# Loading and multiplying the latents' half of x ahead of the context's half in a two-layer transformer block

## The chip, the cores and the metric

The kernel runs on one core of a Trainium2 chip. The metric is the device time of one execution in microseconds (us). Engines are named as in the profile: PE is TensorE (PEld its weight loads), DVE is VectorE, ACT is ScalarE, POOL is GpSimd, SP is SyncE, which issues most loads.

## The reference, cut to what matters

Two layers run over 256 latent tokens (`x`) and 256 context tokens (`ctx`), each of width 1024. What the change touches is the head of layer 0:

```python
sh1, sc1, g1, sh2, sc2, g2 = ada_mod(c, ada_w[0], ada_b[0])          # latents
csh1, csc1, cg1, csh2, csc2, cg2 = ada_mod(c_ctx, ada_w[0], ada_b[0])  # context
h_lat = rms_norm(x, norm1_g[0]) * (1 + sc1) + sh1
h_ctx = rms_norm(ctx, norm1_g[0]) * (1 + csc1) + csh1
# na_mixer: q, k, v = split(h @ w_qkv), first for h_ctx, then for h_lat; attention; w_o
# then swiglu; then layer 1 (a gated scan) and a second swiglu, latents only at the end
```

`ada_mod` is silu(c) times a 1024 x 6144 matrix plus a bias, cut into six modulations. All is float32.

## The kernel before, in words

Activations are held turned: feature block k (128 features, k = 0 to 7) on the partitions, 512 tokens along the free axis, latents in columns 0 to 255 (`LAT`) and context in 256 to 511 (`CTX`). A float32 product is made of three matmuls of split operands (high by high, high by low, low by high), in `prod` at L410. Weights are loaded raw, and `split` makes a high part on ACT (L402) and a low part on DVE (L403).

The program is written against a framework that orders each engine's instructions when the kernel is built, by readiness in its own estimate and by place in the program, and that adds the waits. On the chip each engine takes its list in that fixed order.

`setup` does, in this order of the program: the loads of the two conditioning rows on ACT's queue (`crow`), the four 128-token tiles of `xt` on SP's queue (L93: two of `x`, two of `ctx`), some small rows of biases and gains; the sums of squares of the four tiles on ACT (L107) and one reciprocal root for all four on DVE (`rsqrt`, from L437); the 32 transposes of x on PE (L155) with copies out of PSUM (L156), and among them the eight matmuls that spread the roots over the partitions (L149, L150, copied out as `y0` at L152). Then come four quarters (`qd`). A quarter loads eight blocks of 256 KB of the modulation matrix (`ada_first`, L259) and makes shift and scale for two feature blocks (64 PE instructions at L266 in a single PSUM bank, a copy at L276, a transpose at L277, additions up to L286). It loads three blocks of 256 KB of the q, k and v weights (`w_raw`, L173), splits them, modulates two feature blocks (`modulate`: L363 on DVE, L366 on ACT, L367 on DVE, once for each half of the tokens), and multiplies (`toks`): for each of q, k and v, four token tiles of 128, six matmuls of 256 columns each, so 72 in a quarter. Results gather in six PSUM banks (`early`), two for each of q, k and v: the latents' and the context's.

SP's order is: `xt`, `ada_first` of quarter 0, `w_raw` of quarter 0, `ada_first` of quarter 1, and so on. `ada_first` has 18 buffers.

After `setup` comes `na`, with four groups of heads. Group 0 uses the `early` banks. Its norms of q and k, its table of biases `tb` (loaded by POOL's queue at L535, in pieces of 256 B) and its buffers lie in memory that `setup` held before. Meanwhile the next modulation (`ada`, tiles `ada_raw`, L298, two buffers; PE at L216) and the weights of group 1 (L395) are loaded. High and low weights of q and k have two buffers each: group 1's q weights can be split only when `setup` has done its last product with q's weights.

Of the kernel before, what the change touches and what calls it, by code (L numbers as in the profile page):

```python
# [41 lines left out]
class Block:  # L42
# [25 lines left out]
    def setup(self):  # L68
# [16 lines left out]
        with ExitStack() as ctx:  # L85
# [18 lines left out]
            ss = ip.tile([P, 4], F32, name="ss")  # L104
            junk = ip.tile([P, D], mybir.dt.bfloat16, name="junk")
            for tt in range(4):
                nc.scalar.activation(junk, xt[:, tt], AF.Square, accum_out=ss[:, tt : tt + 1])  # L107
            nc.vector.tensor_scalar(ss, ss, 1.0 / D, EPS, op0=ALU.mult, op1=ALU.add)
            y = self.rsqrt(ss)
# [6 lines left out]
            self.cols = const.tile([P, 2, P], F32, name="cols")  # L116
            cp = self.mixed()
            for j in range(2):
                nc.tensor.transpose(cp[:, j * P : (j + 1) * P], rows[:, j], self.ident)
                nc.vector.tensor_copy(self.cols[:, j], cp[:, j * P : (j + 1) * P])  # L120
# [15 lines left out]
            self.mod = [const.tile([P, 6, KT, 2], F32, name=f"mod{l}") for l in range(2)]  # L136
            self.gs = [const.tile([P, 2, KT, 2], F32, name=f"gs{l}") for l in range(2)]
            self.x = [const.tile([P, T], F32, name=f"x{k}") for k in range(KT)]
            self.hh = [const.tile([P, T], F32R, name=f"hh{k}") for k in range(KT)]
            self.hl = [const.tile([P, T], F32R, name=f"hl{k}") for k in range(KT)]  # L140

            for k in range(KT):
                if k == 4:

                    yb = self.mixed()
                    for tt in range(4):
                        t = slice(tt * P, (tt + 1) * P)
                        dg = ip.tile([P, P], F32, name="dg")
                        nc.vector.tensor_scalar_mul(dg, self.ident, y[:, tt : tt + 1])  # L149
                        nc.tensor.matmul(yb[:, t], self.ones, dg, start=True, stop=True, skip_group_check=True)  # L150
# [930 lines left out]
```

## Time and profile before

| | us |
|---|---|
| runs of the kernel | 1174.02, 1172.62 and one disturbed run of 2835.05; median 1174.02 |
| the profiled execution | 1168.13 |
| its span, first to last instruction | 1166.3 |

The profiled execution is 5.2 us shorter than the mean of the two undisturbed runs, 1173.3. PE's clock was granted in full in nearly the whole span. Times in rows are counted from the span's start.

### The profile page before, as it was taken

How to read it: one execution, taken by the hardware profiler on the slowest of the kernel's cores; microseconds unless marked ns; L12 is line 12 of the kernel's file. 1: busy time of each engine (PE TensorE's matmuls, PEld its weight loads, DVE VectorE, ACT ScalarE, POOL GpSimd, SP SyncE). 2: the span in 40 equal slices, each digit the busy share in tenths (PEclk: the TensorE clock that was granted, in tenths of full speed). 3: DMA queues.
4: the chain of work that ended last, by engine and by line, in shares of the span. 5: the costliest groups of instructions: out<-in, count | busy, mean ns of one | idle time of the engine just before them, and what ended most of it. 6: DMA issues, size and time to landing. Idle time of an engine off the chain costs nothing.

```text
span 1166.3 us, 21342 instructions
## 1 busy us (share of the span) xinstructions
PE 1138.9 (98%) x8539; PEld 987.2 (85%) x8539; DVE 778.7 (67%) x1872; ACT 501.7 (43%) x1079; POOL 74.5 (6%) x121
## 2 busy tenths in 40 slices
PE   6979989999999999999999999999999999999998
PEld 5968869887898787878887889889797988999998
DVE  4579776966697664845353778686768687556553
ACT  5356564745462232213223344434243465545442
POOL 1045331410000000000000000000000000000000
PEclk9999999999999999999999999999999999999999
DMA  9785452433337442636352651323232345564562
GB/s 330 252 211 94 118 131 73 64 130 124 107 93 229 135 170 94 230 136 216 130 194 68 199 167 46 100 74 110 73 110 74 99 175 197 182 210 158 197 217 87
DMA packets 134403, 169.23 MB, mean 145 GB/s; under 512 B 4609, under 2 KB 122273, under 8 KB 134305
## 3 DMA queue, kind: packets, MB, share of 16 engines
q1 hardware_dynamic: 132368, 164.64, 42.5%
q0 software_dynamic: 1728, 3.17, 3.2%
q8 instruction: 67, 1.10, 0.4%
q14 instruction: 32, 0.25, 0.1%
q10 hardware_dynamic: 208, 0.07, 0.0%
HBM read 166.82 MB, written 1.05 MB: 144 GB/s over the span
## 4 chain that ended last, share of the span: by engine, by line
PE 90%; DVE 4%; DMA 3%; ACT 2%; issue 1%; ACTq 0%; DVEq 0%
PE mm L410 49%; PE ax L410 28%; DMA ada_raw<-in_ada_w_dram 3%; PE ada_ps L216 2%; PE ax L651 2%; PE ax L902 1%; PE ax L613 1%; PE ax L579 1%; PE ax L637 1%; PE ax L885 1%; PE ax L580 1%; PE ada_ps L266 1%; ACT qs L569 1%; DVE w_lo L403 1%; PE ax L948 1%; PE ax L659 1%
## 5 line engine op out<-in xcount | busy, mean ns | idle before, releaser
L403 DVE TENSOR_TENSOR w_lo<-w_raw,w_hi 128x512 fp32r<-128x512 f32 (+1 forms) x448 | 272.5, 644 | 128.4 <-ACT w_hi L402 126.0
L402 ACT CAST w_hi<-w_raw 128x512 fp32r<-128x512 f32 (+1 forms) x448 | 238.0, 583 | 230.6 <-PE mm L410 100.3
L410 PE MATMUL mm<-hl,w_hi 128*128 128x256 f32 (+1 forms) x608 | 201.6, 333 | 0.0
L410 PE MATMUL mm<-hh,w_lo 128*128 128x256 f32 (+1 forms) x608 | 201.3, 332 | 0.0
L410 PE MATMUL mm<-hh,w_hi 128*128 128x256 f32 (+1 forms) x608 | 199.1, 329 | 0.0
L410 PE MATMUL ax<-hh,w_lo 128*128 128x256 f32 (+1 forms) x400 | 131.7, 330 | 0.0
L410 PE MATMUL ax<-hh,w_hi 128*128 128x256 f32 (+1 forms) x400 | 131.7, 329 | 0.0
L410 PE MATMUL ax<-hl,w_hi 128*128 128x256 f32 (+1 forms) x400 | 131.3, 328 | 0.0
L410 PE MATMUL mm<-w_hi,hh 128*128 128x256 f32 x448 | 126.3, 282 | 0.8 <-ACT hh L366 0.8
L410 PE MATMUL mm<-w_lo,hh 128*128 128x256 f32 x448 | 125.7, 280 | 0.0
L410 PE MATMUL mm<-w_hi,hl 128*128 128x256 f32 x448 | 125.5, 280 | 0.0
L410 PEld LDWEIGHTS mm<-hl,w_hi 128*128 128x128 f32 x608 | 114.1, 188 | 11.4
L410 PEld LDWEIGHTS mm<-hh,w_lo 128*128 128x128 f32 x608 | 114.0, 188 | 11.3
L410 PEld LDWEIGHTS mm<-hh,w_hi 128*128 128x128 f32 x608 | 113.8, 188 | 10.9 <-ACT hh L366 0.8
L319 DVE SCALAR_TENSOR_TENSOR ada_acc<-ada_raw,cs,ada_acc 128x1024 f32<-128x1024 f32 x63 | 79.0, 1280 | 19.4 <-DMA ada_raw<-in_ada_w_dram 19.2
L410 PEld LDWEIGHTS mm<-w_hi,hh 128*128 128x128 f32 x448 | 84.6, 189 | 5.1 <-issue 3.2
L410 PEld LDWEIGHTS mm<-w_hi,hl 128*128 128x128 f32 x448 | 84.2, 188 | 2.0 <-issue 1.6
L410 PEld LDWEIGHTS mm<-w_lo,hh 128*128 128x128 f32 x448 | 84.2, 188 | 1.8 <-issue 1.4
L410 PEld LDWEIGHTS ax<-hh,w_hi 128*128 128x128 f32 x400 | 75.2, 188 | 7.6 <-ACT w_hi L402 0.8
L410 PEld LDWEIGHTS ax<-hl,w_hi 128*128 128x128 f32 x400 | 75.1, 188 | 7.4
L410 PEld LDWEIGHTS ax<-hh,w_lo 128*128 128x128 f32 x400 | 74.9, 187 | 7.4 <-DVE w_lo L403 0.2
L696 ACT CAST mid_h<-sa 128x512 fp32r<-128x512 f32 (+1 forms) x44 | 22.5, 512 | 92.8 <-DVE sa L693 92.8
(278 smaller groups left out, 2133.3 us busy)
## 6 DMA issues: line engine op xcount, KB each, us to landing
w_raw<-in_ffn_w_in_dram SPq DMA_DIRECT2D x44, 1024.0 KB, 5.1
ada_raw<-in_ada_w_dram SPq DMA_DIRECT2D x80, 512.0 KB, 4.6
w_raw<-in_hg_w_in_dram SPq DMA_DIRECT2D x20, 1024.0 KB, 4.8
w_raw<-in_na_w_qkv_dram SPq DMA_DIRECT2D x9, 1024.0 KB, 5.0
ada_first<-in_ada_w_dram SPq DMA_DIRECT2D x32, 256.0 KB, 5.9
w_raw<-in_ffn_w_out_dram SPq DMA_DIRECT2D x8, 896.0 KB, 4.5
w_raw<-in_ffn_w_out_dram SPq DMA_DIRECT2D x8, 768.0 KB, 4.3
w_raw<-in_ffn_w_out_dram SPq DMA_DIRECT2D x8, 640.0 KB, 4.3
```

Of the source, the lines that this page charges most:

```text
L216: nc.tensor.matmul(ps[32 * j : 32 * j + 32, 0:256], cs[:, k, :], w[:, j * 256 : (j + 1) * 256], start=(k == 0), stop=(k == last), tile_pos ...
L266: nc.tensor.matmul(ps[32 * j : 32 * j + 32, 0:P], self.cs[:, k, :], w[:, j // 2, (j % 2) * P : (j % 2 + 1) * P], start=(k == 0), stop=(k = ...
L319: eng.scalar_tensor_tensor(acc[s], w, c, acc[s], op0=ALU.mult, op1=ALU.add)
L402: self.nc.scalar.copy(wh[:, ks], raw[:, ks])
L403: self.nc.vector.tensor_tensor(wl[:, ks], raw[:, ks], wh.bitcast(F32)[:, ks], op=ALU.subtract)
L410: self.nc.tensor.matmul(out, a, b, start=(start and i == 0 and j == 0), stop=(stop and i == n - 1 and j == 2), skip_group_check=True,)
L569: nc.scalar.activation(cap(qa[half], P - 1, back), src, AF.Copy, scale=self.q_gain[own])
L579: nc.tensor.matmul(ps, qs[a][:, t], ks[a][:, kr], start=True, stop=False, skip_group_check=True)
L580: nc.tensor.matmul(ps, self.ql[a][:, t], ks[a][:, kr], start=False, stop=True, skip_group_check=True)
L613: nc.tensor.transpose(tp[:, kt * P : (kt + 1) * P], sb[:, kt * P : (kt + 1) * P], self.ident)
L651: nc.tensor.matmul(o[64 * a : 64 * a + 64, 0:256], v[:, kt, j * P + 64 * a : j * P + 64 * a + 64], pts[a][0][:, kt], start=(kt == 0), stop ...
L696: nc.scalar.copy(mh, sa)
```

## The change

The two tiles of `ctx` are loaded after the first quarter's modulation blocks and weights, not ahead of them. Squares, root, transposes and spreading are done half by half in a new function `x_turned`: the latents' ahead of the small rows' transposes, the context's inside the first quarter, through PSUM banks that will later hold the context's products. Each quarter's products go first over the latents for q, k and v, then over the context. In quarters 1 to 3 the modulation's matmuls run over the eight blocks from the last to the first. Buffers, weights and arithmetic stay.

```diff
-            for tt in range(4):
-                src = self.in_x if tt < 2 else self.in_ctx
-                nc.sync.dma_start(xt[:, tt], src[0, (tt % 2) * P : (tt % 2 + 1) * P, :])
+            def x_in(half):
+                src = self.in_ctx if half else self.in_x
+                for i in range(2):
+                    nc.sync.dma_start(xt[:, 2 * half + i], src[0, i * P : (i + 1) * P, :])
+
+            x_in(0)
...
+            def x_turned(half, bank):
+                r = HALVES[half][1]
+                ss = ip.tile([P, 2], F32, name="ss", tag=f"ss{half}")
+                junk = ip.tile([P, D], mybir.dt.bfloat16, name="junk", tag="junk")
+                for i in range(2):
+                    nc.scalar.activation(junk, xt[:, 2 * half + i], AF.Square, accum_out=ss[:, i : i + 1])
+                nc.vector.tensor_scalar(ss, ss, 1.0 / D, EPS, op0=ALU.mult, op1=ALU.add)
+                y = self.rsqrt(ss)
+                for k in range(0, KT, 2):
+                    tp = bank()
+                    for b in range(4):
+                        last = nc.tensor.transpose(
+                            tp[:, b * P : (b + 1) * P],
+                            xt[:, 2 * half + b % 2, (k + b // 2) * P : (k + b // 2 + 1) * P],
+                            self.ident,
+                        )
+                    for e in range(2):
+                        nc.any.tensor_copy(self.x[k + e][:, r], tp[:, e * 256 : (e + 1) * 256])
+                yb = bank()
+                for i in range(2):
+                    dg = ip.tile([P, P], F32, name="dg", tag="dg", bufs=2)
+                    nc.vector.tensor_scalar_mul(dg, self.ident, y[:, i : i + 1])
+                    nc.tensor.matmul(
+                        yb[:, i * P : (i + 1) * P], self.ones, dg, start=True, stop=True, skip_group_check=True
+                    )
+                nc.scalar.copy(y0[:, r], yb[:, 0:256])
+                return last
+
+            with self.tc.issue_after(x_turned(0, self.mixed).ins):
...
             self.early = [[self.bank(t) for _ in range(2)] for t in ("mm", "ax0", "ax1")]
+            spare = [banks[1] for banks in self.early] + [self.mm()]
+            turn = iter(spare + spare[:1])
             self.ada_first(ip, 0)
             for qd in range(4):
...
                     self.split(wh, wl, raw, ks)
+                if qd == 0:
+                    x_in(1)
+                    x_turned(1, lambda: next(turn))
                 for k in (2 * qd, 2 * qd + 1):
                     for s, r in HALVES:
                         self.modulate(0, 0, k, s, r, y0[:, r])
                 if qd < 3:
                     self.ada_first(ip, qd + 1)
-                for (raw, wh, wl), banks in zip(ws, self.early):
-                    for tt in range(4):
-                        i = tt % 2
-                        self.toks(
-                            banks[tt // 2][:, i * 256 : (i + 1) * 256], (wh, wl), tt, (2 * qd, 2 * qd + 1),
-                            qd == 0 and i == 0, qd == 3 and i == 1,
-                        )
+                for half in range(2):
+                    for (raw, wh, wl), banks in zip(ws, self.early):
+                        for i in range(2):
+                            self.toks(
+                                banks[half][:, i * 256 : (i + 1) * 256], (wh, wl), 2 * half + i,
+                                (2 * qd, 2 * qd + 1), qd == 0 and i == 0, qd == 3 and i == 1,
+                            )
...
     def ada_first(self, ip, qd):
...
+            tiles.append((k, w))
+
+        for n, (k, w) in enumerate(tiles if qd == 0 else tiles[::-1]):
             for j in range(4):
                 nc.tensor.matmul(
...
-                    start=(k == 0),
-                    stop=(k == KT - 1),
+                    start=(n == 0),
+                    stop=(n == KT - 1),
```

## Rows read from the trace of the kernel before

**Rows 1.** The page, its first part: busy us (share) xinstructions by engine.

```profile
PE 1138.9 (98%) x8539; PEld 987.2 (85%) x8539; DVE 778.7 (67%) x1872; ACT 501.7 (43%) x1079; POOL 74.5 (6%) x121
```

**Rows 2.** Windows view: stretch, busy us (xcount) by engine, clock, DMA share, GB/s.

```profile
21.38:33.00 11.62, 11.62 (x116) 9.81 (x116) 7.97 (x21) 5.05 (x10) 0.00 (x0) 1.00 1.09 359
54.50:62.75 8.25, 8.25 (x73) 8.12 (x72) 4.18 (x7) 4.37 (x8) 0.00 (x0) 1.00 0.11 28
62.75:75.00 12.25, 9.23 (x90) 7.42 (x90) 9.77 (x50) 3.86 (x7) 4.92 (x9) 1.00 1.04 273
75.00:88.00 13.00, 9.96 (x76) 6.26 (x76) 9.63 (x30) 8.43 (x15) 7.53 (x8) 1.00 0.82 207
```

**Rows 3.** Chain of waits in time order, 43 to 87 us: start, us, what.

```profile
43.90 1.88 PE ada_ps L266 x64
...
57.29 5.53 PE ax L410 x48
63.45 4.90 DMA ada_raw<-in_ada_w_dram
...
69.09 9.64 DMA ada_raw<-in_ada_w_dram
```

**Rows 4.** Timeline, SP alone: start, us, what issued xcount.

```profile
4.20 5.81 SPq L259 DMA_DIRECT2D ada_first<-in_ada_w_dram  x8
10.62 1.78 SPq L173 DMA_DIRECT2D w_raw<-in_na_w_qkv_dram  x3
12.79 5.39 SPq L259 DMA_DIRECT2D ada_first<-in_ada_w_dram  x8
...
42.93 17.99 SPq L395 DMA_DIRECT2D w_raw<-in_na_w_qkv_dram  x3
```

**Rows 5.** DMA issues from 4.1, 12.7, 60, 69 and 72 us: KB, us to landing.

```profile
ada_first<-in_ada_w_dram SPq DMA_DIRECT2D x1, 256.0 KB, 6.4
...
ada_first<-in_ada_w_dram SPq DMA_DIRECT2D x1, 256.0 KB, 5.8
...
w_raw<-in_na_w_qkv_dram SPq DMA_DIRECT2D x1, 1024.0 KB, 6.6
...
ada_raw<-in_ada_w_dram SPq DMA_DIRECT2D x1, 512.0 KB, 9.6
...
ada_raw<-in_ada_w_dram SPq DMA_DIRECT2D x1, 512.0 KB, 7.5
```

**Rows 6.** Timeline, 8 to 22 us: start, us, what xcount, [idle before, releaser].

```profile
8.54 1.06 ACT L107 ACTIVATE junk<-xt 128x1024 bf16<-128x1024 f32 x1 [1.84 <-DMA xt<-in_ctx_dram]
...
11.11 0.17 DVE L437 TENSOR_SCALAR rq_y<-ss 128x4 int32<-128x4 int32 x1
...
13.37 0.15 DVE L441 SCALAR_TENSOR_TENSOR rq_y<-rq_b,rq_y 128x4 f32<-128x4 f32 x1
...
14.22 0.71 PE L155 MATMUL mm<-ident,xt 128*128 128x128 f32 x5
...
15.86 0.49 PE L150 MATMUL mm<-dg,ones 128*128 128x128 f32 x2
...
18.62 0.29 DVE L276 COPY ada_row<-ada_ps 128x128 f32<-128x128 f32 x1 [0.89 <-PE ada_ps L266]
...
19.70 0.69 DVE L403 TENSOR_TENSOR w_lo<-w_raw,w_hi 128x512 fp32r<-128x512 f32 x1
...
20.82 0.91 ACT L366 ACTIVATE hh<-ht,mod 128x256 fp32r<-128x256 f32 x2 [1.82 <-DVE ht L363]
...
21.38 0.38 PE L410 MATMUL mm<-w_hi,hh 128*128 128x256 f32 x1 [0.77 <-ACT hh L366]
```

**Rows 7.** Waits of SP's queue, 56 to 90 us: total, times, longest us.

```profile
SPq L395 <- DVE w_lo L403: 12.5, 1, 12.5
```

**Rows 8.** DMA queues, 63 to 88 us: packets, MB, share of 16 engines.

```profile
q1 hardware_dynamic: 2680, 5.11, 60.4%
q0 software_dynamic: 384, 0.79, 30.8%
```

More of the change, by code (lines that the diff above doesn't have):

```diff
@@ L114, in setup @@
             nc.vector.tensor_tensor(self.cs[:, :, 0:2], self.cs[:, :, 0:2], cv, op=ALU.mult)
[L116 to L120, printed above, removed]
+            self.mod = [const.tile([P, 6, KT, 2], F32, name=f"mod{l}") for l in range(2)]
+            self.gs = [const.tile([P, 2, KT, 2], F32, name=f"gs{l}") for l in range(2)]
@@ new lines, in setup @@
+            self.x = [const.tile([P, T], F32, name=f"x{k}") for k in range(KT)]
+            self.hh = [const.tile([P, T], F32R, name=f"hh{k}") for k in range(KT)]
+            self.hl = [const.tile([P, T], F32R, name=f"hl{k}") for k in range(KT)]
+            y0 = ip.tile([P, T], F32, name="y0")
+            def x_turned(half, bank):
[25 more added lines that the diff above has]
+                return last
@@ L121, in setup @@
+            with self.tc.issue_after(x_turned(0, self.mixed).ins):
+                self.cols = const.tile([P, 2, P], F32, name="cols")
+                cp = self.mixed()
+                for j in range(2):
+                    nc.tensor.transpose(cp[:, j * P : (j + 1) * P], rows[:, j], self.ident)
+                    nc.vector.tensor_copy(self.cols[:, j], cp[:, j * P : (j + 1) * P])
             c0, c1 = self.cols[:, 0], self.cols[:, 1]
@@ L134, in setup @@
             nc.vector.tensor_scalar_mul(self.nomlb, self.omlb, -1.0)
[L136 to L150, printed above, removed]
-                    y0 = ip.tile([P, T], F32, name="y0")
-                    nc.scalar.copy(y0, yb)
-                tp = self.mixed()
-                for tt in range(4):
-                    nc.tensor.transpose(tp[:, tt * P : (tt + 1) * P], xt[:, tt, k * P : (k + 1) * P], self.ident)
-                nc.any.tensor_copy(self.x[k], tp)
             wq = self.in_na_w_qkv[0]
@@ L182, in setup @@
                     self.ada_first(ip, qd + 1)
-                for (raw, wh, wl), banks in zip(ws, self.early):
-                    for tt in range(4):
-                        i = tt % 2
-                        self.toks(
-                            banks[tt // 2][:, i * 256 : (i + 1) * 256], (wh, wl), tt, (2 * qd, 2 * qd + 1),
-                            qd == 0 and i == 0, qd == 3 and i == 1,
-                        )
+                for half in range(2):
[5 more added lines that the diff above has]
+                            )
     def masks(self):
@@ L256, in ada_first @@
         ps = self.psum.tile([P, T], F32, tag="ada", name="ada_ps", bufs=1)
+        tiles = []
         for k in range(KT):
```

5 lines of the change are left out of this document (removed).

## The prediction

> **What bounds the kernel now.** I read the page's first part, then the windows by stage, then the chain of waits over the first 90 us, then SP's queue. PE is busy for 1138.9 of 1166.3 us [rows 1], so a change at the head can give back only what PE loses there; whatever is gained must still be there when the long, PE-filled part begins, at about 88 us. The reader is to see three stretches in [rows 2, 3]. Up to 21.38 us PE waits for data: the first product starts then [rows 6]. From 21.38 to 62.75 us PE is never idle (11.62 busy of 11.62, 8.25 of 8.25) [rows 2]. From 62.75 to 88 us it idles again, 3.0 us in the first 12.25 and 3.0 in the next 13 [rows 2], and the chain there is made of `ada_raw` loads: 4.90 us, then 9.64 [rows 3]. In the last stretch of `setup` the DMA engines stand nearly still, 0.11 busy; behind it they are full, 1.04 [rows 2].
>
> **Loads at the head.** Block 1 of quarter 0 lands at 4.20 + 6.4 = 10.6 us, block 1 of quarter 1 at 12.79 + 5.8 = 18.6 [rows 4, 5]. Between them lie 11 loads of 256 KB in 8.0 us: 0.73 us each, 2.9 us for a megabyte. So quarter 0's last block lands at 10.6 + 7 x 0.73 = 15.7, its third weight block at 17.9, quarter 1's last block at 23.7, quarter 2's at 31.7. Taking a megabyte of `ctx` from ahead of quarter 0 moves its last block to 12.8 and its weights to 15.0. The `ctx` tiles then land at 16.4 and 17.9; everything behind lands as before.
>
> **The first product.** Before, PE's modulation is done near 18.6, where the copy starts, 2.9 us after the last block has landed: it stands in PE's list among x's transposes and the spreading of the roots. From the copy to the first product are 21.38 - 18.62 = 2.8 us, of which one DVE split of 0.69 lies in the way [rows 6]. After, PE has only half of x's turning to do and is done with it while blocks land. Eight instructions of the last block are 1.88 / 8 = 0.24 us [rows 3], so the copy starts at 13.1 and the first product comes at 15.2 to 15.9. The third weight block wants 15.0 plus a rounding and a split, about 1.3, so I take **16.0**, 5.4 us sooner.
>
> **What now lies behind it.** A quarter is 72 products at 5.53 / 48 = 0.115 us [rows 3]: 8.3 us, of which the latents' 36 are 4.15. The context's 16 transposes, at (0.71 - 0.27) / 4 = 0.11 with 0.27 for one alone, are 1.8 us, and two spreadings of 0.49 each 1.0 [rows 6]. Those 2.8 us were hidden by the waiting for blocks; now they stand behind the first product. Quarter 1's modulation is 1.9 [rows 3]. The context's chain: second tile landed 17.9; its square 1.06 and the reading of the sum, 19.2; root 13.52 - 11.11 = 2.4 plus one step, 21.8; two spreadings one after the other 1.0; a copy, a DVE and an ACT step of about 0.45 each: **24.2**. The latents' products end at 20.1, the transposes at 21.9, the spreadings near 22.8, so PE waits about 1 us for quarter 1's last block (23.7) and the context. Then 1.9 and 4.15: quarter 0 is done at **29.8**, with both orders of the last two. ACT and DVE have quarter 0's splits and both modulations in the same stretch, so 1 us of queueing may come on top.
>
> **The reversed order.** Before, quarter 1's blocks are multiplied as they land, between products: 21.38 to 33.0 is 11.6 us for 8.3 of products and 1.2 of modulation (40 of 64 instructions), so the changing to and fro costs about 2.1. One run of 64 saves most of that, and it is in the 29.8. Where it costs: the whole run now waits for the block that lands last. For quarter 2 that is 31.7, while PE arrives at 30 to 31; I take 1 us. With it quarter 1 starts about 31 + 1, against 33.0 + 1.9 less what was already done. The gain G that reaches the end of `setup` is then **2.0 us** (29.8 against 33.0 is 3.2, less 1.2 of queueing and waiting). Bounds: at best the first product comes at 15.2 and PE never waits, 15.2 + 4.15 + 2.8 + 1.9 + 4.15 = 28.2, G = 4.8; at worst, see the second rival, G = -1.5. `setup` ends at 62.8 - 2.0 = 60.8.
>
> **Where it goes next.** Two things were waiting for `setup`. POOL's table loads and the next `ada_raw` tiles wait for its end: they come 2.0 sooner. But the third `w_raw` of group 1 waits for DVE, 12.5 us [rows 7]: its raw buffer is free when q's weights of group 1 are split, and those can be split when the last product with group 0's q weights is done. Before, q's 24 products of the last quarter came first and ended at 57.29, 5.53 us ahead of the end; that load was issued at 42.93 + 17.99 - 0.38 = 60.54 [rows 3, 4], 3.25 later. After, q's context products come after all the latents', and only k's and v's context products follow: 24 x 0.115 = 2.8 us ahead of the end. The load goes out at 60.8 - 2.8 + 3.25 = **61.25**, 0.7 us *later* than before, although `setup` ends sooner. From there to the landing of the sixth `ada_raw` tile (issued at about 72.45, 7.5 to land [rows 5]: 80.0) the DMA engines are full [rows 2]. They have the same work to do: SP's queue holds 60.4% and POOL's 30.8% of them [rows 8]. Work that starts all at once at 61.25 to 61.6 and takes as long as before ends 0.7 us later, and PE, which has the modulation of these tiles in its list ahead of group 1's products, waits for them. In numbers the shift at 80 us is 2.8 - G - 0.1, about **+0.7 us**: a gain at the head of less than 2.7 is given back here. G = 4.8 makes it -2.1, G = -1.5 makes it +4.2.
>
> **A rule against the trace.** The 9.6 us of the fifth `ada_raw` tile against 4.9 of the third [rows 3, 5] show that loads of SP and of POOL hold each other up. The Trainium skill says, in "DMA: Bandwidth & Descriptors", section "Queues, rings and completion order", that each DMA engine takes turns between the queues that have work, a packet from each; by that rule table loads that start 2 us sooner delay the megabyte that now starts beside them, which puts the shift on the same side as the sum above, and the rows here agree.
>
> **Rest.** All that follows is PE's list with the same products, so the shift of 0.7 stays: 1168.13 + 0.7 = 1168.8 for the profiled execution. The two undisturbed runs lie at 1173.3 in the mean, 5.2 above it; on their scale that is **1174.0 us**. Buffers, instruction counts and arithmetic outside `setup` are the same; what differs there is only how the scheduler interleaves, worth the few tenths by which single waits in [rows 6] move, and more in 62 to 88 us, where PE's 6 us of idle time bound it: I allow 2 us either way.
>
> **Rivals.**
> *The gain is kept* (0.25). If the stage behind `setup` is not full but a chain of single loads, each issued when PE frees a buffer, all of it moves with the end of `setup`: G of 2 to 4 is kept, 1169 to 1171.5. For it: the chain of waits shows loads following PE there. Against it: DMA 1.04 and the load of 9.64 where a free one takes 4.9 [rows 2, 3].
> *The latents queue behind the context, slower* (0.13). The text of the program has `x_turned(1)` ahead of the first `modulate`, and ACT and DVE take their lists in order. If the context's squares stand ahead of the latents' `hh` on ACT, the latents wait for `ctx`: first product 19.2 + 1 = 20, G near 0, and 1176. If all of the context's turning stands ahead, the first product comes at 24.2 and 8.3 + 1.9 follow, 34.4, G = -1.5: 1177.5. The point that decides: whether the last of the context's squares starts ahead of the first `hh`. Against it: before, the list had each ready piece first (splits between the modulation's copy and `ht`) [rows 6].
> *The clock falls in the new gap* (0.07). From 13.1 to 16 PE has little to do but one transpose. If the granted clock were to fall to its lower level (1.2 GHz of 2.4), products would take 0.23: the latents' 4.15 become 8.3, of which 1 to 2 hide in the wait for the context; G about 0, 1176. Against it: the clock stays at 1.00 through 62.75 to 75 with a quarter of it idle [rows 2]. The Trainium skill's page "TensorE: Matmul & The Clock Gate", Part 1, has the rule that an idle PE is put back to half clock and must earn the full one again; no row here shows it fall.
> *The head does not move* (0.05): the load that was taken away is made up by the wait of new loads for the rows' small ones, G = 0.5, then 1175.5.
>
> **How the numbers follow.** Forecast 0.5, 1172 to 1176 by its own bounds; rivals as above. The range has the kept gain's slower three quarters on one side and the slower rivals up to 1177.5 on the other, with the 0.7 us by which the two undisturbed runs differ from their mean: 1167 to 1178.5, leaving out 2 in 10. Over 2%, about what a measurement of this kernel can tell from no change, would be 23.5 us. No case comes near: 0.02 on each side for a re-ordering of later stages, which all depend on how the scheduler lists them, and 0.96 within.
>
> **What would show it.** In the changed kernel's profile: `ctx` issued behind the first `w_raw`; the first product at 15.5 to 17; the end of `setup` at 59 to 62; the third `w_raw` of group 1 issued within 1 us of 60.5; the first `ada_raw` chain up to 88 us ending within 1.5 us of before. Wrong if the sixth tile's landing moves with `setup`'s end, if the first product comes after 19, if the windows show a clock under 1.00 in 13 to 25 us, or if later stages take another number of us for the same products.

## The result, and the profile of the changed kernel

The changed kernel takes 1181.66 us in the median (1179.35 to 1182.71, five runs) beside 1172.62 us for the kernel before on the same occasion: a ratio of 1.0083, with an interval of 1.0055 to 1.0112. It is slower by 9 to 10 us (6 to 13 by the interval). The forecast was 1174.0 with a range to 1178.5, so the time lies outside it, though within the 2% that held 0.96 of the chance. Two things went worse than the forecast said: the head of the kernel lost time, and the same products took longer in most stages. One went better, in the stage behind `setup`. The slower products have nothing to do with the order of the work.

The page's first part answers to [rows 1]:

```profile
PE 1155.0 (98%) x8539; PEld 1003.1 (85%) x8539; DVE 777.8 (66%) x1886; ACT 501.1 (42%) x1085; POOL 74.4 (6%) x121
```

PE has the same 8539 instructions and is busy for 16.1 us longer than in [rows 1], more than the 14.6 us by which the profiled span grew (1166.3 to 1180.9). So the loss isn't waiting alone: the same instructions take longer. A part of that is the clock, as the windows by stage show (columns as in [rows 2]):

```profile
13.30:18.00 4.70, 1.33 (x5) 0.88 (x5) 3.27 (x13) 3.77 (x8) 0.00 (x0) 0.72 1.03 384
18.00:26.30 8.30, 5.31 (x25) 4.94 (x25) 5.01 (x20) 3.29 (x9) 0.00 (x0) 0.71 1.10 361
26.30:32.50 6.20, 6.17 (x74) 5.33 (x75) 3.92 (x8) 2.42 (x5) 0.00 (x0) 0.50 1.10 357
54.50:68.95 14.45, 14.45 (x124) 14.32 (x124) 3.63 (x8) 3.32 (x7) 0.00 (x0) 1.00 0.01 2
...
76.50:84.70 8.20, 3.25 (x22) 2.34 (x22) 7.26 (x40) 0.60 (x1) 1.68 (x1) 0.73 1.05 270
84.70:90.50 5.80, 5.80 (x30) 4.99 (x31) 0.00 (x0) 0.00 (x0) 4.72 (x7) 0.50 0.93 223
```

The seventh column of numbers is the granted clock. In the kernel before it was 1.00 in all of these stretches. Here it is 0.72, 0.71 and 0.50 from 13.3 to 32.5 us, and 0.73 and 0.50 again from 76.5 to 90.5. Each fall comes in a stretch in which PE stood still for long: it was busy for 1.33 us of 4.70, 5.31 of 8.30, 3.25 of 8.20; the stretch behind it is then paid at half speed. The fourth row is the last stretch of `setup`: PE is full, the DMA engines stand still (0.01).

The last of these falls can't be laid to the change. Of the twenty kernels profiled for this document, the kernel before is the only one without a fall between 70 and 91 us; e17 below, with the same lists of instructions, has one, and so has e1, with nearly the same. The kernel before from 62 to 100 us:

```profile
62.00:100.00 38.00, 31.81 (x261) 23.63 (x259) 31.55 (x115) 19.71 (x41) 19.72 (x26) 1.00 0.82 197
```

And e1_rev_only:

```profile
62.00:100.00 38.00, 32.41 (x249) 24.99 (x247) 30.33 (x108) 18.64 (x39) 19.72 (x26) 0.91 0.83 194
```

Of 91 later runs of the kernel before, only 11 have a mean clock of 1.000. So its profile is of a better execution than most, and the 14.6 us between the profiled spans overstate the loss of 9 to 10 us between the medians.

What PE waited for from 12 to 100 us (us in total, times, longest):

```profile
PE ada_ps L236 <- DMA ada_raw<-in_ada_w_dram: 4.9, 2, 2.9
PE ada_ps L301 <- DVE ada_row L300: 2.7, 1, 2.7
PE mm L434 <- ACT hh L390: 2.2, 2, 1.5
PE mm L145 <- DVE dg L144: 1.5, 1, 1.5
```

DVE's own list says why. This is its timeline (start, us, what, [idle before]); the answers in [rows 6] are the copy of `ada_row` and the split next to it:

```profile
14.12 0.69 DVE L427 TENSOR_TENSOR w_lo<-w_raw,w_hi 128x512 fp32r<-128x512 f32 x1 [3.69 <-ACT w_hi L426]
14.73 0.28 DVE L156 COPY cols<-mm 128x128 f32<-128x128 f32 x1
14.93 0.68 DVE L427 TENSOR_TENSOR w_lo<-w_raw,w_hi 128x512 fp32r<-128x512 f32 x1
...
15.67 0.28 DVE L300 COPY ada_row<-ada_ps 128x128 f32<-128x128 f32 x1
...
16.93 0.48 DVE L387 SCALAR_TENSOR_TENSOR ht<-x,gs,y 128x256 f32<-128x256 f32 x1
...
20.71 0.16 DVE L461 TENSOR_SCALAR rq_y<-ss 128x2 int32<-128x2 int32 x1
...
23.70 0.48 DVE L144 TENSOR_SCALAR dg<-ident,rq_y 128x128 f32<-128x128 f32 x2
25.25 0.88 DVE L387 SCALAR_TENSOR_TENSOR ht<-x,gs,y 128x256 f32<-128x256 f32 x2 [1.07 <-ACT y L148]
```

PE has multiplied the last block at 13.27, so the copy of `ada_row` could start then. In DVE's fixed list two splits, a copy of `cols` and two small operations stand ahead. DVE stands idle for 3.69 us until the first split has its weights, and the copy starts at 15.67. Only feature block 0 of the latents is modulated at once (`ht` at 16.93, first product at 18.01). Block 1 of the latents, which needs nothing of the context, stands behind the context's copies, its root and its spreading, at 25.25. Nine products came in between, and then PE stood still twice for 1.5 us.

The chain of waits from 40 to 95 us, which answers to [rows 3] (start, us, what):

```profile
56.05 10.49 issue
66.54 0.63 ACT w_hi L426
...
69.72 0.37 SPq L419
70.18 0.53 SPq L322
70.83 13.80 DMA ada_raw<-in_ada_w_dram
```

SP's wait from 12 to 100 us, which answers to [rows 7] (total, times, longest):

```profile
SPq L419 <- DVE w_lo L427: 23.5, 2, 17.8
```

`setup` ends at 69.0 instead of 62.8, and the third `w_raw` of group 1 goes out at 69.72 instead of 60.55. It waited 17.8 us for DVE's splits, which waited for q's last products. All loads of the next stage start there, and PE waits for `ada_raw`.

Everything up to here is at the head and right behind it. That it is not all is seen in the middle of layer 0's swiglu, where nothing was edited. The chain of waits there is PE alone; before, 24 products of 512 columns:

```profile
426.11 5.49 PE mm L410 x24
```

and after, 48 of them:

```profile
425.00 11.24 PE ax L434 x48
```

5.49 / 24 is 229 ns for one product, 11.24 / 48 is 234, with the clock at 1.00 in both.

### The profile page after: what moved, and what is told of

Same layout as the page of the kernel before. It is cut to its first block, busy times and chain, and to the rows that moved or that the text cites. A ratio compares the mean times of both kernels' runs of the same rounds, so it can differ in the third digit from the quotient of the medians.

```text
span 1180.9 us, 21372 instructions
## 1 busy us (share of the span) xinstructions
PE 1155.0 (98%) x8539; PEld 1003.1 (85%) x8539; DVE 777.8 (66%) x1886; ACT 501.1 (42%) x1085; POOL 74.4 (6%) x121
## 2 busy tenths in 40 slices
DMA packets 134403, 169.24 MB, mean 143 GB/s; under 512 B 4608, under 2 KB 122272, under 8 KB 134304
## 3 DMA queue, kind: packets, MB, share of 16 engines
q0 software_dynamic: 1728, 3.17, 3.1%
## 4 chain that ended last, share of the span: by engine, by line
PE 89%; DVE 4%; DMA 3%; ACT 2%; issue 1%; SPq 0%; ACTq 0%
PE mm L434 48%; PE ax L434 29%; PE ax L675 2%; DMA ada_raw<-in_ada_w_dram 2%; PE ada_ps L236 1%; PE ax L637 1%; PE ax L603 1%; DVE w_lo L427 1%; PE ax L926 1%; PE ax L604 1%; PE ax L661 1%; PE ax L909 1%; PE ada_ps L290 1%; PE ax L972 1%; PE ax L683 1%
## 5 line engine op out<-in xcount | busy, mean ns | idle before, releaser
L434 PE MATMUL mm<-hl,w_hi 128*128 128x256 f32 (+1 forms) x584 | 196.8, 337 | 0.0
L434 PE MATMUL mm<-hh,w_lo 128*128 128x256 f32 (+1 forms) x584 | 195.9, 336 | 0.1
L434 PE MATMUL mm<-hh,w_hi 128*128 128x256 f32 (+1 forms) x584 | 194.3, 333 | 0.0
L434 PE MATMUL ax<-hl,w_hi 128*128 128x256 f32 (+1 forms) x424 | 139.2, 329 | 0.0
L434 PE MATMUL ax<-hh,w_lo 128*128 128x256 f32 (+1 forms) x424 | 139.1, 329 | 0.0
L434 PE MATMUL ax<-hh,w_hi 128*128 128x256 f32 (+1 forms) x424 | 138.9, 329 | 0.0
L434 PEld LDWEIGHTS ax<-hh,w_hi 128*128 128x128 f32 x424 | 79.6, 188 | 8.5 <-ACT hh L390 0.4
L434 PEld LDWEIGHTS ax<-hl,w_hi 128*128 128x128 f32 x424 | 79.7, 188 | 8.2
L434 PEld LDWEIGHTS ax<-hh,w_lo 128*128 128x128 f32 x424 | 79.7, 188 | 8.2
L434 PE MATMUL ax<-mid_h,w_hi 128*128 128x256 f32 (+1 forms) x222 | 72.8, 328 | 0.0
```

Of the source, the lines that this page charges most:

```text
L434: self.nc.tensor.matmul(out, a, b, start=(start and i == 0 and j == 0), stop=(stop and i == n - 1 and j == 2), skip_group_check=True,)
```

## The experiments

All ratios are to the kernel before on the same occasion, with a 95% interval. The table counts along PE's list of 4608 products with `hh` or `hl`: the end of number 287 is the end of `setup`, number 1152 is the first of layer 0's swiglu. The columns "288 to 1152" (the stage `na`) and "1152 to last" run from start to start, in us. "512" is the mean spacing of products 1632 to 1728 (512 columns, first swiglu), "256" that of 216 to 287 (last quarter of `setup`).

| kernel | ratio | `setup` ends | 288 to 1152 | 1152 to last | 512, ns | 256, ns |
|---|---|---|---|---|---|---|
| before | 1 | 62.8 | 259.7 | 775.1 | 228.9 | 114.7 |
| changed | 1.0083 | 69.0 | 261.8 | 780.4 | 234.2 | 119.3 |
| e1_rev_only | 1.0000 | 62.4 | 263.8 | 774.9 | 228.9 | 114.7 |
| e2_half_only | 0.9975 | 63.4 | 258.2 | 775.0 | 228.9 | 116.5 |
| e3_after_wm | 1.0143 | 67.2 | 264.3 | 780.9 | 234.2 | 117.9 |
| e4_after_lat | 1.0059 | 64.9 | 260.6 | 782.7 | 234.2 | 118.0 |
| e9_after_addr | 0.9990 | 67.7 | 259.6 | 773.2 | 228.9 | 115.0 |
| e10_before_addr | 1.0101 | 63.5 | 265.8 | 782.1 | 234.2 | 119.3 |
| e16_lat_addr | 0.9963 | 62.3 | 260.2 | 772.5 | 228.9 | 114.9 |
| e11_lat_addr_warm | 0.9928 | 60.6 | 259.8 | 773.0 | 228.9 | 115.0 |

The 259.7 us of the kernel before in `na` are those of its better execution, without a fall of the clock in the stage. At its pace e1 has 263.8 and e17 (below, with the same lists) 264.4, so the stage behind `setup` is best held against e1.

### One part of the change alone

The first theory, A in the expectations, had three parts: lists at the head, the clock, and q's weights held by the new product order. **e1_rev_only** is the kernel before with the reversed runs of `ada_first` alone.

```diff
-            for j in range(4):
...
+            tiles.append((k, w))
+
+        for n, (k, w) in enumerate(tiles if qd == 0 else tiles[::-1]):
```

> The kernel before with one part of the change alone: ada_first's matmuls of quarters 1 to 3 are written in the reverse order of their loads, everything else as before. Theory A (the loss comes from the engines' lists at the head, from the clock that falls in the gaps they leave, and from q's weights being held) has nothing here: 1173 us within 2, `setup` ends at 62 to 63.5 us, the granted clock is full from 12.3 us on. Rival B (the reversed run waits for its last block while the products stand behind it in TensorE's list, and that is the loss): `setup` ends at 65 or later, the clock at half in 20 to 33 us, and the median is 1178 to 1182.

1169.91 us, ratio 1.0000 [0.9981, 1.0018]: the reversal neither costs nor gives anything that lasts. Its first product comes at 21.8 and `setup` ends at 62.4; rival B falls.

**e2_half_only** has the new product order alone, and **e12_half_again** repeats it on another occasion.

```diff
-                for (raw, wh, wl), banks in zip(ws, self.early):
-                    for tt in range(4):
+                for half in range(2):
+                    for (raw, wh, wl), banks in zip(ws, self.early):
+                        for i in range(2):
```

> The kernel before with one other part alone: the products of each quarter half by half (q, k, v for the latents, then q, k, v for the context), loads, turn and ada_first as before. Theory A: the head is as before (first product about 21.4 us, clock full from 12.3), `setup` ends within 1 us of 62.75, but q's second half of weights comes free about 5 us later than before (near 60 us), so the third w_raw is issued at 60.5 to 63 and the time is 1173 to 1177. Rival C (the held weights are the whole loss): the third w_raw later than 65 us, PE idle by 3 us or more in 76 to 85 us, and 1179 to 1182.

> The kernel before with the half-by-half product order alone, a second time, on the chip of these runs, so that it can be held against the run above: 1166 to 1169 us, with product 1200 to the last in 768 us. If its earlier 0.9975 was chance, 1170 to 1172.

1167.26 us, 0.9975 [0.9955, 0.9995], and 1167.82 us, 0.9963 [0.9941, 0.9986]. Both theories had this order as a cost; it is a gain of 3 to 4 us. The hold itself is as predicted: the third `w_raw` goes out at 63.91, where the prediction's own rule (end of `setup`, 63.4, less 2.8, plus 3.25) gives 63.9. But it isn't paid for. The stage behind is shorter than in e1, 258.2 against 263.8. Product 576 still starts 0.3 us later than in e1 (135.5 against 135.2), product 672 starts 5.4 us sooner (167.0 against 172.4). PE's waits from 140 to 170 us show one place. The kernel before:

```profile
PE ada_ps L216 <- DMA ada_raw<-in_ada_w_dram: 3.2, 2, 2.6
```

And e2:

```profile
PE ax L637 <- DVE sbc L586: 0.3, 1, 0.3
```

A wait of 3 us near 154 us is gone. The other kernels of the old product order that were profiled have that wait (e1, e6, e10, e13, e15, e17: 1.2 to 3.7 us from 155 to 158 on), and in four of them (e1, e6, e10, e17) the clock is granted at half for some us from 157 to 161 on. So the place of the gain is shown. That the order of the lists in `na` brings the loads forward is only argued; which instruction does it was not followed further.

**e3_after_wm** puts the old product order back into the changed kernel.

```diff
-                for half in range(2):
-                    for (raw, wh, wl), banks in zip(ws, self.early):
+                for (raw, wh, wl), banks in zip(ws, self.early):
+                    for tt in range(4):
```

> The changed kernel with the old product order (q for all four row blocks, then k, then v), everything else as changed. Theory A: the head stays as in the changed kernel or is worse, since q's context products now stand ahead of k's latent products: the gaps and the half clock stay (clock at 1.2 GHz somewhere in 15 to 33 us), `setup` ends at 67 to 70 us, but q's weights come free some 5 us ahead of the end, so the wait at 76.5 to 84.7 us shrinks to under 1.5 us and the clock doesn't fall there: 1176 to 1179. Rival C: the head doesn't matter and the time is back at 1172 to 1174.

1185.92 us, 1.0143 [1.0108, 1.0177]: 4 us worse than the changed kernel by the medians and 7 by the ratios, where theory A had it 3 to 5 better. `setup` does end 1.8 us sooner, but the stage behind takes 264.3 instead of 261.8 and has its wait near 161 us. So the held weights are not the loss.

### The order at the head

**e4_after_lat** traces the latents' two `modulate` calls of quarter 0 first and puts the context's turn behind them.

```diff
-                    x_turned(1, lambda: next(turn))
-                for k in (2 * qd, 2 * qd + 1):
-                    for s, r in HALVES:
-                        self.modulate(0, 0, k, s, r, y0[:, r])
+                    for k in (0, 1):
+                        hh, hl = self.modulate(0, 0, k, 0, LAT, y0[:, LAT])
+                    with self.tc.issue_after(hh), self.tc.issue_after(hl):
+                        x_turned(1, lambda: next(turn))
+                    for k in (0, 1):
+                        self.modulate(0, 0, k, 1, CTX, y0[:, CTX])
```

> The changed kernel with one order changed: the latents' modulation of blocks 0 and 1 is traced ahead of the context's squares, root and turn, and these are put behind it on VectorE and ScalarE. Theory A: all 18 latent products of quarter 0 (times 2 blocks: 36) run in a row from about 17.5 to 22.5 us, the gap before 25 us shrinks from 3 us to under 1.5, the second fall of the clock (25.65 to 32.48 in the changed kernel) is gone or shorter, `setup` ends at 64 to 67 us and the time is 1175 to 1179. Rival D (the clock falls whatever the order, because the engine stood still before 16 us): the clock is at half in two stretches as in the changed kernel, `setup` ends at 68 or later, 1180 to 1183.

1177.14 us, 1.0059 [1.0036, 1.0082]. `setup` ends at 64.9, 4.1 us sooner, the waits of 1.5 us are gone, and one of the two falls of the clock with them (half from 18.1 to 24.9 only). The order is a cause, worth 4 us at the head; e5 and e7 below, timed on one occasion, confirm it in the whole time. The wait for `ada_row` stays (3.0 us), and no run moved that copy ahead of the splits: what it costs is read from the trace alone. But the swiglu stages still take 782.7 us for the same products, against 775.1 before, and no theory so far had that.

### Where the operands lie

The change needs `x`, `hh` and `hl` sooner and so allocates them ahead of `cols`, `q_gain`, `omlb` and `nomlb`. That moves them by 1184 bytes in every partition: `hh0` from byte 37440 to 36256, while `w_hi` stays at 86784 and 94976. 36256 is no multiple of 64, so the first guess was alignment. **e5_after_pad** and **e6_before_unal** put 32 bytes ahead of `x` and 32 behind `hl`, in the changed kernel and in the one before; **e7_after_lat_pad** adds e4's order.

```diff
+            const.tile([P, 8], F32, name="pad0")
             self.x = [const.tile([P, T], F32, name=f"x{k}") for k in range(KT)]
             self.hh = [const.tile([P, T], F32R, name=f"hh{k}") for k in range(KT)]
             self.hl = [const.tile([P, T], F32R, name=f"hl{k}") for k in range(KT)]
+            const.tile([P, 8], F32, name="pad1")
```

> The changed kernel with 32 bytes a partition put ahead of the tiles x, hh and hl and 32 behind them, and nothing else. In the kernel before hh0 lies at byte 37440 of a partition, a multiple of 64; the change makes these tiles ahead of cols, so hh0 lies at 36256, 32 off a multiple of 64. Theory E (address): products are paced 231 ns at 512 columns and 114 at 256 columns before, 234 and 119 after, because of that offset; with the padding the pace of before returns, the stretch from product 1200 to the last product falls from 773.5 us to 768, and the median from 1181.7 to 1175 to 1176.5. Rival F (the pace comes from the order in which PSUM banks are taken, which is shifted too, or from the chip): the pace stays at 234 and the time at 1180 to 1183.

> The kernel before with the same 32 bytes ahead of x, hh and hl and 32 behind: order, loads and banks as before, hh0 now at 37472, 32 off a multiple of 64. Theory E: 512-column products at 234 ns, product 1200 to the last in 773 to 774 us, `setup` ends 0.5 to 1.5 us later, and the median is 1175.5 to 1178. Rival F: nothing moves, 1169 to 1172.

> The changed kernel with the latents' modulation ahead of the context's turn, and with the padding. Theories A and E together: the gain of the order (4.5 us) and that of the address (5.5 to 6.5) add: 1170 to 1172.5, still with one fall of the clock near 18 to 25 us, `setup` ends at 63.5 to 65. Rival G (the gains don't add, the weights of group 1 end last whatever the head does): 1174 to 1177.

e5: 1180.53 us, 1.0089 [1.0067, 1.0111], products at 233.3 ns: not mended. e6: 1179.04 us, 1.0080 [1.0060, 1.0099], 233.3 ns: the kernel before, with no instruction in another place, is slower by 0.8% through 64 bytes of padding. So addresses matter, and a multiple of 64 is not the rule. e7: 1176.39 us, 1.0053 [1.0033, 1.0073]; the order's gain is there (every run of e7, 1174.0 to 1176.8, is faster than every run of e5, 1179.3 to 1180.7), the address's isn't.

The clean pair swaps the addresses alone: **e9_after_addr** is the changed kernel with the small tiles allocated ahead again, **e10_before_addr** the kernel before with `mod`, `gs`, `x`, `hh` and `hl` ahead of `cols`. Every engine's list is that of its parent.

```diff
+            self.cols = const.tile([P, 2, P], F32, name="cols")
+            self.q_gain = const.tile([P, 1], F32, name="q_gain")
+            self.omlb = const.tile([P, 16], F32, name="omlb")
+            self.nomlb = const.tile([P, 16], F32, name="nomlb")
             self.mod = [const.tile([P, 6, KT, 2], F32, name=f"mod{l}") for l in range(2)]
```

> The changed kernel with cols, q_gain, omlb and nomlb allocated ahead of mod, as they were before: every engine's list is that of the changed kernel, and x, hh, hl and the rings of weights lie at the addresses of the kernel before (hh0 at 37440, w_hi at 86784 and 94976). Theory E2 (the pace hangs on where the operands lie, though not on a multiple of 64 alone): 512-column products at 229 ns again, product 1200 to the last in 768 us, and 1174 to 1177 us, 5 to 6 under the changed kernel. Rival F (the order of the banks, or the order of work): 233 to 234 ns, 773 us, 1180 to 1183 us.

> The kernel before with mod, gs, x, hh and hl allocated ahead of cols, so that they lie where the change puts them (hh0 at 36256); every engine's list is that of the kernel before. Theory E2: 512-column products at 234 ns, product 1200 to the last in 773 to 774 us, 1175 to 1180 us. Rival F: 229 ns, 768 us, 1169 to 1172 us.

e9: 1170.48 us, **0.9990** [0.9971, 1.0009]. e10: 1183.67 us, **1.0101** [1.0074, 1.0128]. The chain of waits in the first swiglu, e9:

```profile
419.99 10.99 PE ax L434 x48
```

The same of e10:

```profile
423.37 11.24 PE ax L410 x48
```

229 and 234 ns have changed places, and both times lie outside theory E2's ranges, e9 under its 1174 us and e10 over its 1180. The whole 9 to 10 us by which the changed kernel is slower go away with the old addresses, and the new addresses alone put them on the kernel before. With the old addresses the change is neither faster nor slower. Of the 10.7 us between the spans of the changed kernel and e9, 7.2 lie in the swiglu and scan stages, 2.2 in `na` and 1.3 in `setup`.

Three more runs moved one operand each. **e13_before_w64**: 64 bytes behind `hl`, so the weights lie later. **e14_after_q32**: the changed kernel with `q_gain` alone ahead of `mod`, so `hh` lies 32 bytes later. **e15_before_m64**: `nomlb` behind `hl`, so `hh` lies 64 bytes earlier. **e17_before_all64** then moved `hh` and the weights by 64 together.

```diff
             self.hl = [const.tile([P, T], F32R, name=f"hl{k}") for k in range(KT)]
+            const.tile([P, 16], F32, name="pad")
```

This is e13; e17 has the same line ahead of `self.mod`. In e14 and e15 one line changes its place:

```diff
+            self.q_gain = const.tile([P, 1], F32, name="q_gain")
             self.mod = [const.tile([P, 6, KT, 2], F32, name=f"mod{l}") for l in range(2)]
...
-            self.q_gain = const.tile([P, 1], F32, name="q_gain")
```

```diff
-            self.nomlb = const.tile([P, 16], F32, name="nomlb")
...
             self.hl = [const.tile([P, T], F32R, name=f"hl{k}") for k in range(KT)]
+            self.nomlb = const.tile([P, 16], F32, name="nomlb")
```

> The kernel before with 64 bytes put behind hl: x, hh and hl stay (hh0 at 37440), the rings of weights and all that follows lie 64 bytes later (w_hi at 86848 and 95040, no longer multiples of 128). Theory J (the weights' address matters too, so the padding of the earlier runs spoiled one operand while it mended the other): 512-column products at 232 to 234 ns and 1175 to 1180 us. Rival K (only hh's and hl's address matters): 229 ns and 1169 to 1172 us.

> The changed kernel with q_gain alone allocated ahead of mod: x, hh and hl lie 32 bytes later (hh0 at 36288, a multiple of 64 and not of 128, as 37440 is), the weights and all else where the change has them. Theory J (multiples of 64 for hh and hl and multiples of 128 for the weights are enough): 229 ns, product 1200 to the last in 765 to 768 us, 1168 to 1172 us. Rival L (it is the distance between the operands or a larger block of addresses that counts): 232 to 234 ns and 1178 to 1182 us.

> The kernel before with nomlb allocated behind hl: x, hh and hl lie 64 bytes earlier (hh0 at 37376, a multiple of 128), weights as before. If a multiple of 64 is enough for hh, 229 ns and 1169 to 1172 us. If a multiple of 128 is better still, under 228 ns and 1160 to 1168. If the distance to the weights counts, 232 to 234 ns and 1175 to 1182.

> The kernel before with 64 bytes ahead of mod: x, hh, hl, the weights and all that follows lie 64 bytes later, so the distance from hh0 (37504) to w_hi (95040) is 57536 bytes as in the kernel before. The last two address runs, one with the weights 64 later and one with hh and hl 64 earlier, have the same distance of 57600 and the same pace (226.7, 120.0 and 119.2 ns). Theory M (the distance between the two operands of a product sets the pace): 228.9 ns at 512 columns, 117.8 in the last stage, 114.7 in the last quarter of `setup`, as before, and 1168 to 1172 us. Rival N (the place of either operand counts by itself): another pace, 1174 us or more.

The chain of e13 in the first swiglu:

```profile
419.48 10.88 PE ax L411 x48
```

Of e15:

```profile
419.81 10.88 PE ax L410 x48
```

Of e14:

```profile
421.89 11.20 PE ax L434 x48
```

And of e17:

```profile
419.17 10.99 PE ax L411 x48
```

| kernel | `hh0`, `w_hi` | distance | 512, ns | 256 in the last stage, ns | 256 in `setup`, ns | ratio |
|---|---|---|---|---|---|---|
| before | 37440, 94976 | 57536 | 228.9 | 117.8 | 114.7 | 1 |
| e17_before_all64 | 37504, 95040 | 57536 | 228.9 | 117.8 | 115.1 | 1.0025 [1.0008, 1.0043] |
| e13_before_w64 | 37440, 95040 | 57600 | 226.7 | 120.0 | 119.2 | 1.0075 [1.0050, 1.0100] |
| e15_before_m64 | 37376, 94976 | 57600 | 226.7 | 120.0 | 119.2 | 1.0057 [1.0038, 1.0075] |
| e14_after_q32 | 36288, 94976 | 58688 | 233.3 | 113.3 | 117.6 | 1.0038 [1.0022, 1.0055] |
| changed | 36256, 94976 | 58720 | 234.2 | 117.3 | 119.3 | 1.0083 |

None of the first three came out in full as a theory had it: e13 and e15 have a faster pace at 512 columns and lose time all the same, and e14 has the slow pace of rival L and loses only 0.4%. Its 32 bytes take back about half of the change's loss. Moving the weights 64 bytes up and moving `hh` 64 bytes down give the same pace, to a tenth of a nanosecond in three places; moving both together gives the pace of the kernel before, to 0.4 ns in the third. So, in the kernel before, the pace of a run of products went with the distance between its two operands and not with the place of either. The distance 57600 is better than that of before where `hh` streams with 512 columns and worse with 256 columns, and it loses on the whole. What is left open is the rule that turns a distance into a pace, and what in the chip does it. e17's 1.0025 is small but not quite nothing. The distance isn't all, either. e4 has the addresses of the changed kernel and from product 1152 on the same list of PE, yet it has 120.0 ns in the last stage for 117.3, and 782.7 us from there to the last for 780.4. In the same way e5 (233.3 ns at 512 columns) and e7 (232.4) share 58752. And each kernel has one profile, so whether its pace changes from one execution to the next is not shown.

### The clock

**e8_lat_pad_warm** is e7 with TensorE kept busy where it stood: 12 products behind quarter 0's `ada_first` and 4 behind its transposition. **e11_lat_addr_warm** has the same with the old addresses, **e18_lat_addr_warm_again** repeats it, and **e16_lat_addr** is e11 without the added products.

```diff
+        if qd == 0:
+            for _ in range(12):
+                nc.tensor.matmul(self.warm[:, 0:P], self.ones, tiles[-1][1][:, 0, 0:P],
+                                 start=True, stop=True, skip_group_check=True)
         row = self.spool.tile([P, 256], F32, name="ada_row", tag="ada_row", bufs=1)[:, 0:P]
```

> The same with TensorE kept busy where it stood: 12 products of ones with the last ada_first block behind the ada_first matmuls, and 4 of ones with ada_row behind the transposition, all into a bank that is written over later; they add work and nothing to the result. Theory H (the clock falls because TensorE stood still near 14 to 17 us): the granted clock stays full through 12 to 33 us and the products of quarter 0 run at 0.12 us; `setup` ends 1.5 to 3.5 us earlier than without, at 61 to 63 us, and the median is 1167 to 1170. Rival I (the clock falls for another reason, such as the small share of the array that ada_first's 32-row matmuls use): the clock falls as before and the time is that of the run without, or up to 1 us above it.

> The changed kernel with the latents' modulation ahead of the context's turn and the addresses of the kernel before, without the added products that kept TensorE busy. If the fall of the clock near 17 to 25 us costs what the pair at the other addresses showed (2.6 us), it is 1166.5 to 1169 us, with one stretch at half clock before 33 us and `setup` ending 1 to 3 us later than with the added products (60.3 for product 287). If the clock costs nothing that lasts, 1163.5 to 1165.5.

> The changed kernel with all three repairs: the latents' modulation ahead of the context's turn, TensorE kept busy from 13 to 17 us by 16 added products, and the addresses of the kernel before. If the three causes are the whole loss, `setup` ends at 60.5 to 62 us (1 to 2 ahead of before), the pace is 229 ns and the median is 1165 to 1169. If something of the change still costs (q's weights held, so that group 1 comes late), it is 1170 to 1172.5 with a wait for ada_raw of over 4 us in 70 to 90 us.

> The fastest version so far (the latents' modulation ahead of the context's turn, TensorE kept busy, the addresses of the kernel before) a second time beside the kernel before on another occasion: 1162 to 1167 us and a ratio of 0.990 to 0.996. If the first result was a lucky chip, 0.997 or above.

The windows of e7 (columns as in [rows 2]):

```profile
12.50:17.70 5.20, 1.69 (x13) 0.87 (x13) 3.67 (x13) 2.56 (x6) 0.00 (x0) 0.86 1.05 384
17.70:23.50 5.80, 5.74 (x28) 5.74 (x29) 4.55 (x19) 3.62 (x9) 0.00 (x0) 0.54 1.10 348
```

And of e8:

```profile
12.50:19.50 7.00, 6.57 (x70) 5.70 (x63) 4.61 (x16) 3.73 (x7) 0.00 (x0) 1.00 1.07 373
19.50:21.60 2.10, 2.10 (x20) 2.10 (x19) 2.00 (x8) 2.07 (x7) 0.00 (x0) 1.00 1.11 349
```

With PE busy for 6.57 of 7.00 us instead of 1.69 of 5.20, the clock stays at 1.00 and the first 16 products take 2.0 us instead of 5.8. e8's first product comes later than e7's, 19.6 against 17.8, and its `setup` ends 1.1 us sooner; 1173.78 against 1176.39 us on one chip. The clock does what theory H said; the gain of 1.1 us in `setup` is under its range of 1.5 to 3.5, and the time is above its range, since the addresses were not mended. At the old addresses e16 takes 1166.83 us, 0.9963 [0.9944, 0.9981]; e11 1164.56 us, 0.9928 [0.9903, 0.9953]; e18 1164.57 us, 0.9944 [0.9921, 0.9968]. All three comparisons give the added products 2 to 4 us, but in each of them the intervals overlap. The Trainium skill has this in "TensorE: Matmul & The Clock Gate", Part 1, "HAM oscillation — how this bites in real kernels": an engine that stands still between bursts is put back to half clock and pays again. The trace agrees: 0.54 in the second row of e7, 1.00 in e8. The later falls between 70 and 91 us remain in all of these kernels.

e11 has the order, the clock and the addresses repaired together and beats both kernels: the one before by 6 to 8 us and the changed one, on another occasion, by 17. Its `setup` ends at 60.6 (61.5 in e18); the prediction had 60.8 for the change.

## Why the prediction was wrong, point by point

**Loads at the head: right.** The latents' loads and quarter 0's blocks came as predicted: the last block landed at 12.8 and the context's first tile at 16.1 (16.4 predicted); its second was there by 17.87, when its square starts.

**The first product: 16.0 predicted, 18.0 measured.** The step that failed is "the copy starts at 13.1". It took the time at which PE is done as the time at which DVE starts. The copy started at 15.67: DVE's fixed list had other work ahead, which waited for weights that landed later than the last block (13.4 against 12.8). The sum had put just one split in the way.

**What lies behind the first product: wrong.** The sum let the latents' 36 products run in one go to 20.1. Nine came, and the rest waited for the context, because half of the latents' modulation stood behind the context's chain in DVE's list. The second rival had the mechanism, but its deciding point, "whether the last of the context's squares starts ahead of the first `hh`", did not decide: the last square starts at 17.87, after the first `hh` at 17.45, and the rival happened all the same to the second feature block, on DVE. A chance of 0.13 for it was too low, since the program's text has the context's turn first, and the one row cited against it [rows 6] was of a list with another program's text.

**The clock: held for 0.07.** It fell twice at the head. The row cited against it (1.00 from 62.75 to 75 us with a quarter of the stretch idle) was no bound for a stretch with 1.33 us busy of 4.70, and it came from the one profile in which the clock did not fall there: in e1 it is at half from 72 to 79 us. At equal addresses, keeping the clock up at the head came out as 2 to 4 us (0.9963 against 0.9928 and 0.9944), with intervals that overlap.

**G, the gain that reaches the end of `setup`: +2.0 predicted, -6.2 measured**, outside the bounds of 4.8 and -1.5, which had no clock and no address in them. Of the 8.2 us between the two, e9, e16, e11 and e18 take apart 7.5 to 8.4, by the profiled executions: 1.3 for the addresses (69.0 to 67.7), 5.4 for the order and the waits and clock that go with it (67.7 to 62.3), 0.8 to 1.7 for what the clock still cost (62.3 to 60.6 in e11 and 61.5 in e18). With those repaired, G is 1.3 to 2.2.

**The third `w_raw`: the mechanism right, the price of the wrong sign.** The product order holds q's weights, and the load goes out where the rule puts it (e2: 63.91). "The shift of 0.7 stays" was the step that failed: the same order removes a wait of 3 us at 154 us. Alone it gains 3 to 4 us, where the sum charged it about 0.7. The reading that loads of SP and POOL hold each other up was not shown by its rows either: the fifth `ada_raw` tile (9.64 us) was in flight beside a megabyte of SP's own, issued at 64.38 and landed at 77.5.

**"Buffers, instruction counts and arithmetic outside `setup` are the same": true of their size and number, and not enough.** This is the step that cost the forecast: where the tiles lie was a term put at nothing. The prediction said it would be wrong "if later stages take another number of us for the same products", and they did: 780.4 us against 773.2 in the pair that differs in addresses alone. The moved allocations stand in the diff of the kernel, and no term of the sum was theirs. Swapping them back takes the whole loss away (0.9990), and they alone cost the kernel before 1.0% (1.0101).

**The range.** Its words and its numbers don't agree: 1167 lies under all of the kept gain's 1169 to 1171.5, so no quarter of that rival is left out, and of the 2 in 10 that are said to lie outside only the 0.04 beyond 2% is named. The addresses, which carried the time past 1178.5, were no rival at all.

**Put together.** With the addresses of before the change gives 0.9990 [0.9971, 1.0009]. Beside e1, e9 loses 5.3 us at the head (67.7 against 62.4), gains 4.2 in `na`, where the wait is gone, and gains 1.8 from product 1152 on (773.2 against 774.9), which no run took apart. So "no change" came out for the order of the work, but by luck: a loss and gains that the sum did not have cancel. The addresses then made the kernel slower.

## What to carry to other kernels

When an edit moves an allocation, hold the tiles' addresses fixed, or measure the edit with the addresses swapped back: here 1184 bytes cost 9 to 10 us, twice the best gain that the forecast allowed (4.8). Where engines take fixed lists, an operation starts when the list reaches it, so price a moved step by what the list puts ahead of it and not by its inputs; and a gap that is opened ahead of a burst of products is paid for a second time through the clock. A list order that holds a buffer longer may still pay for itself in a later stage, so parts of a change are worth timing one by one.

## What the runs showed of the hardware that was not expected

With nothing but the operands' places changed, the spacing of back-to-back products at full clock differs by 3% at 512 columns (226.7 to 234.2 ns, the list of the kernel before) and by 5% at 256 columns in the last stage (113.3 in e14 to 118.7 in e5, the list of the changed kernel). Within a run the spacings repeat in a fixed pattern, every 3 products at 57536 (232, 226, 229 ns) and every 7 at 58720 (231, 234, 235, 233, 232, 237, 238 ns). What makes the pattern stays open. The Trainium skill says in "TensorE: Matmul & The Clock Gate", Part 2, "Step-by-step: what each phase is for", that TensorE reads the streaming operand and the next weights through two ports of their own, so that loading weights takes nothing from the running product. No run here shows the ports; but with identical lists the pace went with the distance between these two operands, so in this kernel the rule isn't enough to make a product's time independent of where its operands lie.
